# A hybrid attention layer in one kernel: reordering the twelve products behind the two value projections, their weight loads, and the engine of their low parts

## The chip, the core and the metric

The kernel runs on one NeuronCore of a Trainium2 chip. The metric is the device time of one execution in microseconds. The kernel before took 984.92 us (median of 3 runs, 984.27 to 985.51).

The engines have two names each, since the profile uses the short ones: TensorE (PE, with PEld for its weight loads), VectorE (DVE), ScalarE (ACT), GpSimd (POOL) and SyncE (SP). Each engine works through its own instructions strictly in the order of the program. SP issues nearly all DMAs, also in the order of the program: an issue that waits for a free buffer holds up every issue behind it.

## What is computed

One layer of a streaming encoder over 1,024 prompt rows and 64 sample rows of 1,024 columns, in float32. Cut to what matters here:

```python
h = rms_norm(x, norm_w) @ w_in                  # (1088, 1024) @ (1024, 6144)
sb_q, sb_k, sb_v, sb_z, cb_q, cb_k, cb_v, cb_z, g_sb, g_cb = split(h, SPLIT_POINTS)
o_sb = stick_breaking(sb_q, sb_k, sb_v)         # causal, plus caches for the sample rows
o_cb = band_attention(norm(cb_q), norm(cb_k), cb_v, rel_bias)
h = sigmoid(g_sb) * (o_sb * silu(z_sb)) @ w_proj_sb + sigmoid(g_cb) * (o_cb * silu(z_cb)) @ w_proj_cb
return x + h @ w_out, and the new k and v of both branches
```

The part that changes is the columns of `sb_v` (1024 to 1536) and `cb_v` (3072 to 3584) of the first product.

## The kernel before

**Split products.** TensorE multiplies in a fast float32 format with fewer bits. So each operand is kept as a high part (ScalarE rounds it, `A.activation(h, src, AF.Copy)`) and a low part (`src - h`), and each product is three matmuls: high by high, low by high, high by low.

**Seven products instead of eight.** From the values of a block on, the big products go by Strassen's scheme in Winograd's form: a 2 by 2 block product takes seven block products of sums of blocks. For x these sums are four tiles t0 to t3 (L180 to L227, `make_t`). t0 and t1 are made early. t1's unsplit value is stored to DRAM (`d_t1`), and the second half of `make_t` fetches it back eight times, k = 0 to 3 for t2 and then for t3: each of these eight jobs takes two subtractions or additions by VectorE, the high part by ScalarE and the low part by VectorE (`put_t`, L174). The generator is advanced at fixed places of the program, in the list `TJ` for its last nine steps: the first of them only fetches, the other eight are the jobs. A job of the kernel before fetches for the job two ahead, behind its own work, into the buffer that it has just read (two buffers, name `d`).

**The stage of this change** (L684 to L816) works on two "pairs" j: j = 0 is `sb_v`, j = 1 is `cb_v`. Of the seven products of each pair the first one (left block 0) has been made earlier, and the stage does five, numbered s = 1, 2, 6, 4, 5 by their left operand (`LEFT`, L712: s = 1 takes t1, s = 2 takes t0, s = 6 a half of x itself, s = 4 takes t2, s = 5 takes t3), while s = 0 is a small product of the sample rows alone (`sample`, 8 matmuls). The list `ORDER` (L713) fixes their sequence. A product has four parts, numbered 2c + tt, of 12 matmuls of 128 columns of weights by 256 columns each. At the head of each part `part((q, 2c+tt))` (L727) does what the program places there: sums of raw weight quarters (`sum_w`, VectorE), splits of a weight block into high and low part (`split_quad`, L510: high by ScalarE, low by GpSimd unless an engine is given), loads, and jobs of `make_t`. q is the place in `ORDER`. Behind each half c of a product, `evac_p` takes the result out of PSUM by VectorE, and for s of 3 and more `put_v` stores it.

**Weights.** A weight quarter of this stage is a tile of 128 by 4 by 256 float32 (512 KB), `quad[j, h, w]`: h the half of rows, w the half of columns. Written below as q_jhw. The pool `wpool` has two buffers `wraw` for them, `natx` one (`wrawx`), and a pool `rw` (r11, r00, r10), opened where the pools of the stage before are closed, has three more. The second pair's sums are made at (4, 0) to (4, 3). For splits, pool `wpool` and pool `natx` take turns.

**The stage ahead of it.** Products of the normed q and k columns run at L623 to L682, each followed by a norm, and three products later by a transpose (`post_nat`, L394: two transposes by TensorE, high part by ScalarE, low part by VectorE, stores at the fourth and eighth tile). The last four transposes fall into the parts (0, 0) to (0, 3). In them the PSUM tile is always `pk`, with one buffer.

**The opening.** At L540 to L610 tiles of x arrive (`load_x`), are normed and transposed, and the first products follow each tile. A list of places counted in matmuls (`SCALE`, `READY`, L562 to L591) says where the next x tile is scaled (`prep_a`, VectorE), transposed (`prep_b`) or its squares are summed (`prep_s`, ScalarE). Two loads of later weight blocks, `load_nat(1, 1)` and `load_nat(2, 0)`, stand ahead of this loop.

Of the kernel before, what the change touches and what calls it, by code (L numbers as in the profile page):

```python
# [34 lines left out]
def hybrid_step_kernel(ctx: ExitStack, tc: tile.TileContext, x_prompt, x_sample, c_sbk, c_sbv, c_cbk, c_cbv,  # L35
# [71 lines left out]
    turn = [0]  # L107

    def shifted(pool, shape, odd):

        o = 0 if turn[0] % 2 == odd else 32
        turn[0] += 1
        t = pool.tile([128, 1056], F32R, name="wlox", bufs=2)[:, o:o + 1024]
        if len(shape) == 4:
            return t.rearrange("p (s k n) -> p s k n", s=shape[1], k=shape[2])
        return t.rearrange("p (k n) -> p k n", k=shape[1])

    class Weights:
# [10 lines left out]
        def hi(self, key, cuts=1):  # L129
            raw, pool, shape, extra = self.raw[key]  # L130
            h = pool.tile(shape, F32R, name="whi" + extra, bufs=2)
# [3 lines left out]
            self.sp[key] = (h, None)  # L135

        def lo(self, key, eng=None):
# [3 lines left out]
            (eng or G).tensor_tensor(out=l, in0=raw, in1=h[:].bitcast(F32), op=OP.subtract)  # L141
# [36 lines left out]
    def make_t(tm, pool):  # L178
# [35 lines left out]
        fetch(*late[1])  # L214
        yield
        for e, (n, k) in enumerate(late):
            d = got[n, k]
            if n == 2:
# [6 lines left out]
            if e + 2 < 8:  # L225
                fetch(*late[e + 2])
# [3 lines left out]
    with ExitStack() as ph:  # L230
# [163 lines left out]
        def post_nat(i, t, qn):  # L394
# [4 lines left out]
            if t in (8, 4):  # L399
                hl[0] = p1h.tile([128, 2, 2, 576], F32R, name="hl", bufs=3)  # L400
            h = hl[0]
            n = 0 if raw1[:2] == (nb - 1, 7) else t % 3
            pt = (psQ.tile([128, 512], F32, name=f"b2{n - 1}")[:, :256].rearrange("p (j n) -> p j n", j=2) if n else
                  psK.tile([128, 2, 128], F32, name="pk"))
# [5 lines left out]
            A.activation(h[:, :, 0, o], pt[:, :, :r], AF.Copy)  # L410
            V.tensor_tensor(out=h[:, :, 1, o], in0=pt[:, :, :r], in1=h[:, :, 0, o].bitcast(F32), op=OP.subtract)
# [63 lines left out]
        def prep(n):  # L475
# [17 lines left out]
            elif s in (2, 4):  # L493
                t = natx.tile(shape, F32R, name="whix", bufs=2)
            else:
                t = wpool.tile(shape, F32R, name="whi" if s == 5 else "wlo", bufs=2)
# [13 lines left out]
        def split_quad(q, src, eng=None):  # L510
# [3 lines left out]
            h = pool.tile([128, 4, 256], F32R, name="whi" + x, bufs=2)  # L514
            A.activation(h, src, AF.Copy)
            l = shifted(pool, [128, 4, 256], 0) if x else pool.tile([128, 4, 256], F32R, name="wlo", bufs=2)
            (eng or G).tensor_tensor(out=l, in0=src, in1=h[:].bitcast(F32), op=OP.subtract)
# [35 lines left out]
        load_nat(1, 1)  # L553
        load_nat(2, 0)
# [10 lines left out]
        def early(at):  # L565
            if at in SCALE:
                p = SCALE.index(at) + 2
                prep_a(QO[p])
                if p + 3 < 9:
                    load_x(QO[p + 3])  # L570
            elif at in READY:
# [4 lines left out]
            elif at == 62:  # L576
                W.split((1, 0), V)
            elif at == 88:
# [44 lines left out]
        for i in range(2, nb):  # L623
# [4 lines left out]
            for ti, t in enumerate(TO):  # L628
# [14 lines left out]
                if ti in (3, 6):  # L643
                    h = ti // 6
                    if i + 1 < nb:
# [3 lines left out]
                        elif h == 0:  # L649
                            load_quad(0, 0, 1, wpool, "wraw", 2)  # L650
                        else:
                            load_quad(0, 1, 1, wpool, "wraw", 2)
# [3 lines left out]
                if (i, ti) == (nb - 1, 2):  # L656
                    for n in (1, 2):
                        made[n] = pn.tile([128, 4, 256], F32, name=f"made{n}", bufs=1)
                    sum_w(made[1], quad[0, 0, 1], quad[0, 1, 1], OP.add)
                if (i, ti) == (nb - 1, 4):  # L660
# [52 lines left out]
        ORDER = [(0, 1), (0, 2), (0, 6), (0, 0), (0, 4), (1, 1), (1, 2), (1, 6), (1, 0), (1, 4), (0, 5), (1, 5)]  # L713
        TJ = [(0, 2), (1, 1), (1, 3), (2, 1), (2, 3), (7, 0), (7, 2), (9, 0), (9, 2)]
        BANKS = {0: "2", 2: "1", 4: "3", 5: "2", 6: "1", 7: "1", 9: "2"}
        u, banks = {(0, "2"): s1t[0]}, {}

        def evac_p(j, s, c, ps):
            two = lambda v: v[:, 2 * c:2 * c + 2].rearrange("p t n -> p (t n)")
            if s < 3:  # L720
                V.tensor_tensor(out=two(u[j, "23"[s - 1]]), in0=ps, in1=two(u[j, "2"]), op=OP.add)
# [5 lines left out]
        def part(at):  # L727
# [3 lines left out]
            if at == (0, 2):  # L731
# [1151 lines left out]
```

## Time and profile before

| | |
|---|---|
| median of 3 runs | 984.92 us |
| lowest, highest | 984.27, 985.51 us |
| the profiled execution: its own time | 984.18 us |
| its span from first to last instruction | 982.0 us |
| TensorE busy (PE) | 954.2 us, 97% of the span |
| VectorE, ScalarE, GpSimd busy | 598.1, 499.3, 404.5 us (61%, 51%, 41%) |
| mean granted TensorE clock | 0.988 |
| DMA | 182.78 MB, mean 186 GB/s |

How to read it: all durations below come from the one profiled execution. Its time is 0.74 us below the median. Matmuls are pipelined, so the records of two neighbours overlap; the pace of a run of matmuls is its stretch of time divided by their number, not the duration of one. The granted clock is the share of the full TensorE clock in a stretch. In rows of waits the columns are total us, number of times and longest us. In rows of windows they are the length, then busy us and number of instructions of PE, PEld, DVE, ACT and POOL, then the granted clock, the DMA share and GB/s.

### The profile page before, as it was taken

How to read it: one execution, taken by the hardware profiler on the slowest of the kernel's cores; microseconds unless marked ns; L12 is line 12 of the kernel's file. 1: busy time of each engine (PE TensorE's matmuls, PEld its weight loads, DVE VectorE, ACT ScalarE, POOL GpSimd, SP SyncE). 2: the span in 40 equal slices, each digit the busy share in tenths (PEclk: the TensorE clock that was granted, in tenths of full speed). 3: DMA queues.
4: the chain of work that ended last, by engine and by line, in shares of the span. 5: the costliest groups of instructions: out<-in, count | busy, mean ns of one | idle time of the engine just before them, and what ended most of it. 6: DMA issues, size and time to landing. Idle time of an engine off the chain costs nothing.

```text
span 982.0 us, 20507 instructions
## 1 busy us (share of the span) xinstructions
PE 954.2 (97%) x7547; PEld 905.2 (92%) x7547; DVE 598.1 (61%) x1164; ACT 499.3 (51%) x1151; POOL 404.5 (41%) x395
## 2 busy tenths in 40 slices
PE   8899999598999999999999999999999999999998
PEld 8899999598999999999999988788888888999998
DVE  5646766765555555544332187778677766389745
ACT  6656766121444333343333276667887776465220
POOL 3156665262545465665543210001331111596641
PEclk9899999898999999999999999999999999999999
DMA  8537665526465655565532897789699851762642
GB/s 268 191 132 273 224 240 209 188 90 226 136 196 164 185 166 156 175 188 175 159 108 85 227 255 207 194 218 237 204 276 280 231 156 59 247 204 92 201 142 85
DMA packets 177705, 182.78 MB, mean 186 GB/s; under 512 B 30713, under 2 KB 160125, under 8 KB 177478
## 3 DMA queue, kind: packets, MB, share of 16 engines
q1 hardware_dynamic: 166182, 166.60, 56.9%
q10 hardware_dynamic: 8608, 8.20, 2.6%
q0 software_dynamic: 2816, 6.69, 2.1%
q8 instruction: 60, 0.98, 0.4%
q14 instruction: 39, 0.32, 0.1%
HBM read 117.79 MB, written 63.64 MB: 185 GB/s over the span
## 4 chain that ended last, share of the span: by engine, by line
PE 85%; DVE 5%; issue 3%; ACT 3%; DMA 1%; POOL 1%; ACTq 0%; DVEq 0%; POOLq 0%
PE b L943 30%; PE acc L560 8%; PE o L1465 7%; PE z L1368 7%; PE pt L1421 7%; PE b L1790 6%; PE acc L1219 5%; PE b L1261 5%; PE acc L1112 5%; PE b L811 3%; DMA xt<-in_x_prompt_dram 1%; PE b L560 1%; DVE d L222 1%; PE acc L1833 1%; DVE xn L312 1%
## 5 line engine op out<-in xcount | busy, mean ns | idle before, releaser
L1421 PE MATMUL pt<-ident,be 128*128 128x128 f32 (+1 forms) x568 | 87.1, 277 | 0.9 <-ACT wT L1430 0.6
L1390 DVE TENSOR_TENSOR_SCAN be<-be,imp 128x128 f32<-128x128 f32 (+7 forms) x64 | 82.8, 1341 | 8.3 <-ACT be L1371 8.3
L1368 PE MATMUL z<-ks,sq 128*128 128x320 f32 (+5 forms) x384 | 87.7, 338 | 0.0
L1430 ACT ACTIVATE wT<-pt 128x512 f32<-128x512 f32 (+3 forms) x123 | 57.2, 499 | 44.2 <-PE pt L1421 44.1
L1421 PEld LDWEIGHTS pt<-ident,be 128*128 128x128 f32 (+1 forms) x568 | 66.2, 140 | 13.8 <-issue 5.3
L943 PE MATMUL b<-xm,wlox 128*128 128x256 f32 (+1 forms) x336 | 76.0, 286 | 0.0
L951 DVE TENSOR_TENSOR u<-b,s 128x256 f32<-128x256 f32 (+1 forms) x56 | 24.3, 440 | 73.4 <-PE b L943 70.1
L1368 PEld LDWEIGHTS z<-ks,sq 128*128 128x128 f32 x384 | 63.5, 190 | 2.2 <-ACT be L1371 0.8
L1465 PE MATMUL o<-wT,vp 128*64 128x256 f32 (+1 forms) x608 | 64.1, 356 | 0.0
L1465 PEld LDWEIGHTS o<-wT,vp 128*64 128x64 f32 x608 | 40.3, 136 | 22.3 <-issue 5.4
L943 PEld LDWEIGHTS b<-xm,wlox 128*128 128x128 f32 x336 | 56.8, 188 | 0.0
L1393 ACT ACTIVATE be<-be,sm 128x640 f32<-128x640 f32 (+5 forms) x68 | 47.2, 694 | 17.7 <-DVE sm L1392 17.6
L1016 POOL DMA_DIRECT2D d_osb<-zt x20 | 10.8, 541 | 100.7 <-DVE zt L1479 43.9
L498 POOL TENSOR_TENSOR whix<-ws,whix 128x512 fp32r<-128x512 f32 x28 | 36.9, 1319 | 34.6 <-ACT whix L497 29.2
L1371 ACT ACTIVATE be<-z 128x384 f32<-128x384 f32 (+6 forms) x104 | 48.3, 521 | 3.4 <-PE z L1368 2.9
L498 POOL TENSOR_TENSOR wlo<-ws,wlo 128x512 fp32r<-128x512 f32 x28 | 38.9, 1388 | 25.5 <-ACT wlo L497 23.2
L1381 ACT ACTIVATE be<-be,sm 128x640 f32<-128x640 f32 (+5 forms) x68 | 47.3, 696 | 3.8 <-DVE sm L1373 3.3
L1261 PE MATMUL b<-og,whi 128*128 128x384 f32 (+1 forms) x192 | 46.7, 326 | 0.0
L845 ACT ACTIVATE hl<-u 128x256 f32<-128x256 f32 (+1 forms) x40 | 16.9, 431 | 55.3 <-DVE u L963 17.8
L943 PE MATMUL b<-t0h,whix 128*128 128x256 f32 (+1 forms) x224 | 44.6, 289 | 0.0
L943 PE MATMUL b<-t3h,whi 128*128 128x256 f32 (+1 forms) x224 | 44.5, 289 | 0.0
L386 ACT ACTIVATE qn<-qn,rsn 128x64 f32<-128x64 f32 (+1 forms) x144 | 38.2, 339 | 11.6 <-POOL rsn L294 11.4
(438 smaller groups left out, 3331.4 us busy)
## 6 DMA issues: line engine op xcount, KB each, us to landing
wraw<-in_w_in_dram SPq DMA_DIRECT2D x33, 512.0 KB, 4.9
wrawx<-in_w_in_dram SPq DMA_DIRECT2D x16, 512.0 KB, 4.3
sq<-d_qsbT SPq DMA_DIRECT2D x32, 192.0 KB, 5.0
sq<-d_qcbT SPq DMA_DIRECT2D x32, 192.0 KB, 4.9
xt<-in_x_prompt_dram SPq DMA_DIRECT2D x8, 512.0 KB, 4.6
d_kcbT<-hl SPq DMA_DIRECT2D x8, 512.0 KB
d_qcbT<-hl SPq DMA_DIRECT2D x8, 512.0 KB, 5.1
d_ksbT<-hl SPq DMA_DIRECT2D x16, 256.0 KB, 3.4
```

The lines of the kernel that those rows point to most:

```text
L498: G.tensor_tensor(out=t[:, 1], in0=src, in1=t[:, 0].bitcast(F32), op=OP.subtract)
L560: TE.matmul(ps, x, w, start=first, stop=last, skip_group_check=i < 2)
L943: TE.matmul(ps[:, :m], w[:, hl_, k], right[s](x)[:, k, a:b], start=s < 3 and k == 0 and e == 0, stop=k == 3 and e == 2, skip_group_check=s ...
L1112: TE.matmul(ps[:, :b - a], w[:, k], xk(x, k)[:, a:b], start=k == 0 and n == 0, stop=k == KT - 1 and n == 2)
L1219: TE.matmul(ps[:, :e - a], w[:, p, cw], g[:, a:e], start=m % 12 == 0, stop=m % 12 == 11)
L1261: TE.matmul(pp[uu][:, :n], w[:, p, uu * 128:uu * 128 + 128], g[:, a:e], start=p == 0 and m == 0, stop=p == NPAIR - 1 and m == 2)
L1368: TE.matmul(z[:, :m], s[:, e, q0:q0 + 128], ks[:, h, o + x:o + y], start=(e, h) == parts[0], stop=(e, h) == parts[-1])
L1390: V.tensor_tensor_scan(be[:r, n - 1::-1], be[:r, n - 1::-1], im[:, ::-1], 0.0, op0=OP.mult, op1=OP.max)
L1421: TE.transpose(pt[:kr, x, :r], be[:r, kb * 128:kb * 128 + kr], ident[:r, :r])
L1430: A.activation(w[:, sl:sl + m, q0:q0 + r], pt[:, :m, :r], AF.Copy)
L1465: TE.matmul(o[hd * 64:hd * 64 + 64, c0:c1], vv[:kr, kb, hd * 64:hd * 64 + 64], wT[b, p, j, hd, s // 4][:kr, s % 4, c0:c1] if j < 4 else wT ...
L1790: TE.matmul(ps[:, t], left[s](xs_, k)[:, ts_], wt_[:, k], start=s < 3 and t == k == e == 0, stop=k == 3 and e == 2, skip_group_check=s > 2 ...
```

## The change

- `ORDER`: the second pair's products s = 2, 1 and 6 come ahead of the first pair's s = 4, which needs t2; the second pair's s = 5 comes ahead of the first pair's. `TJ` spreads the eight jobs differently, and each job fetches for the next one ahead of its own work.
- The second pair's sums and splits move forward to (1, 3) to (4, 1). The splits of places 2, 4 to 10 give their low part to VectorE; those of q_001 and q_011 (the keys 3 and 11) stay with GpSimd.
- Loads: q_011 is loaded ahead of q_001, q_111 takes its buffer in the stage before, q_011 is loaded a second time at (7, 1) (in place of q_111 before), q_101 comes at (0, 3), and `rw` holds q_100, q_110 and two sums.
- `evac_p` takes the results of the second pair's s = 2 out of PSUM together with those of s = 1. Some banks change.
- The last four transposes of `post_nat` use the two-buffer tile `pt`.
- In the opening, `load_nat(1, 1)` moves behind a load of an x tile at 24 matmuls, and `load_nat(2, 0)` to 62 matmuls.
- High parts named `whix` get the same alternating offset of 32 columns that low parts named `wlox` had.

```diff
 def fetch / late half of make_t
         fetch(*late[0])
-        fetch(*late[1])
         yield
         for e, (n, k) in enumerate(late):
             d = got[n, k]
+            if e < 7:
+                fetch(*late[e + 1])
...
-            if e + 2 < 8:
-                fetch(*late[e + 2])
             yield
 post_nat
-            n = 0 if raw1[:2] == (nb - 1, 7) else t % 3
-            pt = (psQ.tile(...b2{n - 1}...) if n else psK.tile([128, 2, 128], F32, name="pk"))
+            if raw1[:2] == (nb - 1, 7):
+                pt = psT.tile([128, 4, 128], F32, name="pt")
...
 opening
-        load_nat(1, 1)
-        load_nat(2, 0)
...
                     load_x(QO[p + 3])
+                if p == 2:
+                    load_nat(1, 1)
...
             elif at == 62:
                 W.split((1, 0), V)
+                load_nat(2, 0)
 the stage before
-                            load_quad(0, 0, 1, wpool, "wraw", 2)
+                            load_quad(0, 1, 1, wpool, "wraw", 2)
                         else:
-                            load_quad(0, 1, 1, wpool, "wraw", 2)
+                            load_quad(0, 0, 1, wpool, "wraw", 2)
...
                     sum_w(made[1], quad[0, 0, 1], quad[0, 1, 1], OP.add)
+                    load_quad(1, 1, 1, wpool, "wraw", 2)
 the stage
-        ORDER = [(0, 1), (0, 2), (0, 6), (0, 0), (0, 4), (1, 1), (1, 2), (1, 6), (1, 0), (1, 4), (0, 5), (1, 5)]
-        TJ = [(0, 2), (1, 1), (1, 3), (2, 1), (2, 3), (7, 0), (7, 2), (9, 0), (9, 2)]
-        BANKS = {0: "2", 2: "1", 4: "3", 5: "2", 6: "1", 7: "1", 9: "2"}
+        ORDER = [(0, 1), (0, 2), (0, 6), (0, 0), (1, 2), (1, 1), (1, 6), (0, 4), (1, 0), (1, 4), (1, 5), (0, 5)]
+        TJ = [(0, 2), (1, 1), (2, 3), (4, 2), (5, 0), (6, 2), (7, 0), (7, 3), (9, 0)]
+        BANKS = {0: "2", 2: "1", 4: "3", 5: "2", 6: "1", 7: "3", 9: "2"}
...
-                V.tensor_tensor(out=two(u[j, "23"[s - 1]]), in0=ps, in1=two(u[j, "2"]), op=OP.add)
+                for e in ((s,) if j == 0 else (1, 2) if s == 1 else ()):
+                    V.tensor_tensor(out=two(u[j, "23"[e - 1]]), in0=banks[j, e, c], in1=two(u[j, "2"]), op=OP.add)
...
-            if at == (0, 2):
+            if at == (0, 0):
                 split_quad(3, quad[0, 0, 1])
...
-            elif at == (0, 3):
+            elif at == (0, 2):
                 sum_w(quad[0, 1, 0], quad[0, 1, 0], made[2], OP.subtract)
...
+            elif at == (0, 3):
+                sum_w(quad[0, 0, 0], quad[0, 0, 0], quad[0, 0, 1], OP.subtract)
+                load_quad(1, 0, 1, wpool, "wraw", 2)
             elif at == (1, 0):
...
-                split_quad(2, quad[0, 1, 0])
-            elif at == (1, 1):
-                sum_w(quad[0, 0, 0], quad[0, 0, 0], quad[0, 0, 1], OP.subtract)
-                split_quad(4, quad[0, 0, 0])
-                load_quad(1, 0, 1, wpool, "wraw", 2)
+                split_quad(2, quad[0, 1, 0], V)
             elif at == (1, 2):
...
-                for h, w in ((1, 1), (0, 0), (1, 0)):
+                for w, h in ((0, 0), (0, 1)):
                     load_quad(1, h, w, rw, f"r{h}{w}", 1)
...
+            elif at == (1, 3):
+                for n in (1, 2):
+                    made[n] = rw.tile([128, 4, 256], F32, name=f"r{n}", bufs=1)
+                sum_w(made[1], quad[1, 0, 1], quad[1, 1, 1], OP.add)
+                split_quad(4, made[1], V)
+            elif at == (2, 1):
+                sum_w(made[2], made[1], quad[1, 0, 0], OP.subtract)
+            elif at == (2, 2):
+                split_quad(5, made[2], V)
             elif at == (4, 0):
-                sum_w(quad[1, 1, 1], quad[1, 0, 1], quad[1, 1, 1], OP.add)
-                made[2] = rw.tile([128, 4, 256], F32, name="r2", bufs=1)
-                sum_w(made[2], quad[1, 1, 1], quad[1, 0, 0], OP.subtract)
-                split_quad(5, made[2])
-            elif at == (4, 2):
-                split_quad(6, quad[1, 1, 1])
+                sum_w(quad[1, 1, 0], quad[1, 1, 0], made[2], OP.subtract)
+            elif at == (4, 1):
+                split_quad(6, quad[1, 1, 0], V)
+            elif at == (5, 1):
+                split_quad(7, quad[0, 0, 0], V)
+            elif at == (5, 3):
                 made[3] = natx.tile([128, 4, 256], F32, name="wrawx", bufs=1)
                 sum_w(made[3], quad[1, 0, 0], quad[1, 0, 1], OP.subtract)
-            elif at == (4, 3):
-                sum_w(quad[1, 1, 0], quad[1, 1, 0], made[2], OP.subtract)
-                split_quad(7, quad[1, 1, 0])
             elif at == (6, 0):
-                split_quad(8, quad[1, 0, 1])
                 rwx.close()
                 open_t((3,))
-            elif at == (7, 0):
-                split_quad(9, made[3])
-            elif at == (7, 3):
-                split_quad(10, quad[0, 1, 1])
-                load_quad(1, 1, 1, wpool, "wraw", 2)
+                split_quad(8, quad[1, 0, 1], V)
+            elif at == (6, 3):
+                split_quad(9, made[3], V)
+            elif at == (7, 1):
+                split_quad(10, quad[1, 1, 1], V)
+                load_quad(0, 1, 1, wpool, "wraw", 2)
+            elif at == (7, 2):
                 load_raw(0)
-            elif at == (9, 2):
-                split_quad(11, quad[1, 1, 1])
+            elif at == (9, 1):
+                split_quad(11, quad[0, 1, 1])
                 load_raw(1)
                 load_raw(2)
```

More of the change, by code (lines that the diff above doesn't have):

```diff
@@ L105, in hybrid_step_kernel, with shifted @@
     wpool = ctx.enter_context(tc.tile_pool(name="wp", bufs=2))
[L107 to L113, printed above, removed]
+    turn = {}
+    def shifted(pool, shape, odd, name="wlox"):
+        n = turn[name] = turn.get(name, 1) + 1
+        o = 0 if n % 2 == odd else 32
+        t = pool.tile([128, 1056], F32R, name=name, bufs=2)[:, o:o + 1024]
         if len(shape) == 4:
@@ L130, in hi @@
             raw, pool, shape, extra = self.raw[key]
-            h = pool.tile(shape, F32R, name="whi" + extra, bufs=2)
+            h = shifted(pool, shape, 0, "whix") if extra else pool.tile(shape, F32R, name="whi", bufs=2)
             for j in range(cuts):
@@ L134, in hi @@
                 A.activation(h[:, k], raw[:, k], AF.Copy)
-            self.sp[key] = (h, None)
+            self.sp[key] = (h[:], None)
         def lo(self, key, eng=None):
@@ L140, in lo @@
             l = shifted(pool, shape, 0) if extra else pool.tile(shape, F32R, name="wlo", bufs=2)
-            (eng or G).tensor_tensor(out=l, in0=raw, in1=h[:].bitcast(F32), op=OP.subtract)
+            (eng or G).tensor_tensor(out=l, in0=raw, in1=h.bitcast(F32), op=OP.subtract)
             self.sp[key] = (h, l)
@@ L401, in post_nat @@
             h = hl[0]
-            n = 0 if raw1[:2] == (nb - 1, 7) else t % 3
-            pt = (psQ.tile([128, 512], F32, name=f"b2{n - 1}")[:, :256].rearrange("p (j n) -> p j n", j=2) if n else
-                  psK.tile([128, 2, 128], F32, name="pk"))
+            if raw1[:2] == (nb - 1, 7):
+                pt = psT.tile([128, 4, 128], F32, name="pt")
+            elif t % 3:
+                pt = psQ.tile([128, 512], F32, name=f"b2{t % 3 - 1}")[:, :256].rearrange("p (j n) -> p j n", j=2)
+            else:
+                pt = psK.tile([128, 2, 128], F32, name="pk")
             for j in range(2):
@@ L409, in post_nat @@
             o = slice(c, c + r)
-            A.activation(h[:, :, 0, o], pt[:, :, :r], AF.Copy)
-            V.tensor_tensor(out=h[:, :, 1, o], in0=pt[:, :, :r], in1=h[:, :, 0, o].bitcast(F32), op=OP.subtract)
+            A.activation(h[:, :, 0, o], pt[:, 0:2, :r], AF.Copy)
+            V.tensor_tensor(out=h[:, :, 1, o], in0=pt[:, 0:2, :r], in1=h[:, :, 0, o].bitcast(F32), op=OP.subtract)
             dst = (d_kT if isk else d_qT)["cb"]
@@ L493, in prep @@
             elif s in (2, 4):
-                t = natx.tile(shape, F32R, name="whix", bufs=2)
+                t = shifted(natx, shape, 0, "whix")
             else:
@@ L513, in split_quad @@
             pool, x = ((wpool, ""), (natx, "x"))[n % 2]
-            h = pool.tile([128, 4, 256], F32R, name="whi" + x, bufs=2)
+            h, l = (shifted(pool, [128, 4, 256], 1, part + x) if x else
+                    pool.tile([128, 4, 256], F32R, name=part, bufs=2)[:] for part in ("whi", "wlo"))
             A.activation(h, src, AF.Copy)
-            l = shifted(pool, [128, 4, 256], 0) if x else pool.tile([128, 4, 256], F32R, name="wlo", bufs=2)
-            (eng or G).tensor_tensor(out=l, in0=src, in1=h[:].bitcast(F32), op=OP.subtract)
+            (eng or G).tensor_tensor(out=l, in0=src, in1=h.bitcast(F32), op=OP.subtract)
             comb[q] = h, l
@@ L649, in hybrid_step_kernel @@
                         elif h == 0:
+                            load_quad(0, 1, 1, wpool, "wraw", 2)
+                        else:
                             load_quad(0, 0, 1, wpool, "wraw", 2)
-                        else:
-                            load_quad(0, 1, 1, wpool, "wraw", 2)
                             load_quad(0, 0, 0, natx, "wrawx", 1)
@@ L800, in hybrid_step_kernel @@
             for c in range(2):
-                if s != 5:
-                    banks[j, c] = None
                 for tt in range(2):
@@ L805, in hybrid_step_kernel @@
                     if tt == 0 and s != 5:
-                        banks[j, c] = psF.tile([128, 512], F32, name="acc") if q == 1 else bank_of(BANKS[q], c)
-                    ps = banks[j, c]
+                        banks[j, s, c] = psF.tile([128, 512], F32, name="acc") if q == 1 else bank_of(BANKS[q], c)
+                    ps = banks[j, 4 if s == 5 else s, c]
                     o = ps[:, 256 * tt:256 * tt + 256]
```

## The prediction

> **What bounds the kernel now.** I read the chain that ended last first, then who waits for TensorE's work, then the changed stretches alone.
>
> ```profile
> PE 85%; DVE 5%; issue 3%; ACT 3%; DMA 1%; POOL 1%; ACTq 0%; DVEq 0%; POOLq 0%
> ```
>
> TensorE carries the chain, so a change is worth what it takes out of TensorE's idle time and slow clock. The waits of PE between 155 and 245 us, the stretch of the ten products:
>
> ```profile
> PE b L811 <- ACT t2h L175: 8.9, 3, 6.2
> PE b L811 <- ACT t3h L175: 4.0, 1, 4.0
> PE pk L406 <- DVE hl L411: 1.5, 1, 1.5
> ```
>
> The same stretch as one window, one window behind the long wait and one around the start of the second; then two pieces of the chain:
>
> ```profile
> 161.22:244.13 82.91, 67.82 (x522) 65.39 (x523) 52.29 (x59) 19.46 (x30) 30.21 (x14) 0.90 0.57 186
> 186.59:193.42 6.83, 0.62 (x2) 0.33 (x2) 2.27 (x4) 0.66 (x1) 0.00 (x0) 0.50 0.57 214
> 224.13:227.55 3.42, 1.40 (x12) 1.20 (x11) 3.42 (x3) 0.86 (x1) 2.34 (x1) 1.00 1.05 355
> 67.37 2.83 PE acc L560 x24
> 244.13 14.94 PE b L943 x120
> ```
>
> The stage ends at 244.13, where the next products (L943) begin. Its 512 matmuls and 8 transposes at the undisturbed pace of 0.118 us (2.83 per 24) need some 61.3 us, and take 82.9. PE is idle for 82.9 - 67.8 = 15.1 of them, and the rest of the 21.6 is the clock: granted 0.50 after the long wait and 0.90 over the stage. It waits first for t2 in the first pair's s = 4, then for t3 in its s = 5. The third loss, 1.5 us, lies just ahead of 161.22: the first of the last four transposes waits for the single buffer `pk`.
>
> The other stretch is the opening, in the chain:
>
> ```profile
> 0.75 4.02 DMA xt<-in_x_prompt_dram
> 15.77 7.09 DMA xt<-in_x_prompt_dram
> 22.96 1.15 ACT sq L303 x2
> 24.11 0.96 ACT whi L134
> 25.15 1.08 issue
> 27.11 1.32 PE pt L322 x8
> 28.43 5.09 PE b L560 x24
> 33.76 0.87 PE pt L322 x8
> ```
>
> The fifth x tile takes 7.09 us to land, where the very first took 4.02. Then ScalarE's squares, its high part, VectorE's low part and scaling follow, and only then the transposes at 27.11. The 24 matmuls from 28.43 take 5.09 us, 0.212 each: half the clock.
>
> **The opening.** SP's issues, the last work of ScalarE ahead of its wait, and three windows:
>
> ```profile
> 13.25 0.39 SPq L126 DMA_DIRECT2D wrawx<-in_w_in_dram  x1
> 13.68 0.50 SPq L126 DMA_DIRECT2D wraw<-in_w_in_dram  x1
> 15.77 0.37 SPq L256 DMA_DIRECT2D xt<-in_x_prompt_dram  x1
> 20.31 0.60 ACT L328 ACTIVATE xm<-pt 128x512 fp32r<-128x512 f32 x1
> 22.75:26.16 3.41, 0.21 (x2) 0.01 (x1) 1.07 (x1) 2.64 (x5) 0.74 (x2) 1.00 0.06 25
> 26.16:29.58 3.42, 2.47 (x13) 2.22 (x14) 2.32 (x5) 1.50 (x3) 0.00 (x0) 0.50 0.49 143
> 29.58:32.99 3.41, 3.41 (x17) 3.41 (x17) 2.12 (x3) 1.64 (x4) 0.74 (x2) 0.50 0.22 88
> ```
>
> The x tile queues behind 1 MB of weights that are split only at 88 and 166 matmuls, while its own place is 24. The change puts it first; its issue stays at 15.77 (its buffer comes free then). At the first tile's 4.02 it lands by 19.8, and ScalarE takes it up when `xm` is done: the second of two 0.5 us steps behind 20.31, so at 20.8. Everything up to the transposes moves by 22.96 - 20.8 = 2.1 us. In the windows PE does 0.21 us, then 2.47 of 3.42, and is still at 0.50 in the third; with PE back at 25.0 the second window is full. If one full window lifts the clock, half speed ends at 29.6 instead of 33. That would save one more us. The same chain then sets the next tile's transposes (33.76 before): PE back at 25.0, 1.3 of transposes, and again 1.15 of squares, 0.96 of high part, 1.08 of low part and 0.88 to the transposes make 30.4. Between ends of 2.0 (clock as before) and 3.3 I take **-3.0**, since from there to 159 every wait is counted from PE's own places. The moved loads are covered: issued near 16 and 20 and landing in 4 to 7 us by the two rows above, they are there long before their splits; uncovered, each would cost its landing.
>
> **The start of the stage.** With two buffers the transposes start 1.5 us earlier, at 159.7: **-1.5**. The last of the four still needs the norm of the last tile, which ScalarE ends about as PE gets there; the split of key 3 moved to (0, 0) puts 1 us of ScalarE ahead of it.
>
> **The stage.** PE no longer meets s = 4 early, so both waits in the first three rows go. What is late next? The change puts eight low parts onto VectorE and keeps its sums, jobs and evictions, so I lay out VectorE's queue. Prices:
>
> ```profile
> 159.60 1.23 DVE L517 TENSOR_TENSOR wlox<-made,whix 128x1024 fp32r<-128x1024 f32 x1 [1.42 <-ACT whix L515]
> 193.84 1.22 DVE L438 TENSOR_TENSOR r<-wraw,r 128x1024 f32<-128x1024 f32 x1
> 179.49 0.71 DVE L219 TENSOR_TENSOR d<-d,xa 128x544 f32<-128x544 f32 x1
> 182.33 0.68 DVE L721 TENSOR_TENSOR made<-acc,made 128x512 f32<-128x512 f32 x1
> 182.93 0.71 DVE L219 TENSOR_TENSOR d<-d,xa 128x544 f32<-128x544 f32 x1
> 225.31 2.73 DVE L222 TENSOR_TENSOR d<-xm,d 128x544 f32<-128x544 f32 x1
> 225.13 2.34 POOL L517 TENSOR_TENSOR wlox<-wraw,whix 128x1024 fp32r<-128x1024 f32 x1 [3.12 <-ACT whix L515]
> L515 ACT ACTIVATE whi<-wraw 128x1024 fp32r<-128x1024 f32 x3 | 3.1, 1047 | 0.0
> ```
>
> A sum or a low part holds VectorE for 1.15 (its end overlaps the next), 1.1 more where it waits for a high part just begun; a job 2.85 (179.49 to 182.33, ScalarE's high part inside); an eviction 0.6. A two-input operation beside GpSimd's low part takes 2.73 instead of 0.71, so moving those parts off GpSimd also removes such meetings; they are left out of the list except for key 3 at the start. Landings (the second and third row are from the DMA issues of 160 to 245 us, with the median time to landing):
>
> ```profile
> 160.86 0.38 SPq L508 DMA_DIRECT2D made<-in_w_in_dram  x1
> made<-in_w_in_dram SPq DMA_DIRECT2D x1, 512.0 KB, 4.4
> d_qcbT<-hl SPq DMA_DIRECT2D x4, 512.0 KB, 5.1
> 179.00 0.33 SPq L211 DMA_DIRECT2D d<-d_t  x1
> 179.50 1.48 SPq L508 DMA_DIRECT2D r<-in_w_in_dram  x3
> 181.03 0.50 SPq L757 DMA_DIRECT2D u<-d_s  x1
> 182.43 3.76 SPq L211 DMA_DIRECT2D d<-d_t  x2
> 190.39 0.72 DVE L219 TENSOR_TENSOR d<-d,xa 128x544 f32<-128x544 f32 x1 [3.94 <-DMA d<-d_t]
> ```
>
> From 179.00 to the landing at 190.3 the queue moved 272 + 3 x 512 + 512 + 272 = 2,592 KB in 11.3 us; loads land in the order of issue. That is the price of a backlog: 0.44 us per 100 KB, latency inside.
>
> On the old clock, without the opening's 3 us: q_010, issued at 160.86 as now, lands at 165.3, and key 3's low part on GpSimd ends soon after. From 165.6 VectorE does two sums, an eviction, the low part of key 2 (170.0), job 0 (172.8), an eviction, and waits for q_101, which queues behind two stores of 512 KB: issued near 167.4, they take 5.1, and q_101 another 2.2, so 174.7. Then: sum and split 4 to 178.2, sum and split 5 to 182.3 with two evictions in its gaps, job 1 and an eviction 185.7, sum and split 6 189.2, jobs 2 and 3 194.9, split 7 196.3, two evictions, a sum, two evictions 199.8, split 8 201.0, an eviction, job 4 204.4, split 9 205.9, an eviction, job 5 209.3, split 10 210.7, an eviction, job 6 and an eviction 214.8. Job 7 needs a fetch that SP issues only behind the second load of q_011, which waits for split 10's low part. At 210.9 that puts 512 (q_011) + 512 (stores) + 512 (raw 0) + 272 KB on the queue: 7.9 us, landing 218.9. Job 7 ends at 221.7, and the eviction behind it at 222.3.
>
> PE, unhindered from 159.7, wants split 4 at 178.5 (there by 0.3), split 5 at 184.2, split 6 at 189.8 (by 0.6), split 7 at 195.5: 0.9 late. Split 9 at 203.0: 3.0 late. It reaches the second pair's s = 5 at 213.2, which adds onto banks that VectorE must have read: 222.4, a wait of **9.2 us**, in place of waits of 6.2 and 4.0. It then runs below full clock for two windows (2.3 us lost, from the 0.50 rows) and ends the remaining 96 + 16 matmuls (13.2 us) at **237.9**, against 244.13: -6.2, of which 1.5 were counted above, so **-4.7**. The last stores' buffers hold back the fold of the samples and, behind it on ScalarE, the third weight block of the next stage: +0.3, between 0 and 1.
>
> The bank swaps, the deferred eviction (two in a row, counted) and the offset of `whix` add no instruction. The q_111 load in the stage before follows a sum there; it delays no wait that I see.
>
> Sum: -3.0 - 1.5 - 4.7 + 0.3 = -8.9. The profiled execution took 984.18 (span 982.0 and 2.2 around it), so 975.3 of its own; the median shown lies 0.74 above it, so the forecast is **976.0**.
>
> **A rule weighed.** The row has GpSimd's low part at 2.34 and VectorE's at 1.23. The Trainium skill (GPSIMD Engine Reference, 4.1 Engine selection) recommends VectorE for such elementwise work since GpSimd takes about twice as long for two inputs; this trace agrees on the ratio. Taken as the whole answer, the rule makes each late part sooner and gives the first rival below; the list above says that VectorE's queue is already the late one.
>
> **Rivals.** *VectorE keeps up* (or the last fetch lands early): with none of these waits the stage would end at 159.7 + 61.3 = 221.0 at best, total 984.2 + 0.7 - 3.0 - 23.1 = 959; without the fetch's 4.1 us and its slow clock alone, 970. For it: the prices carry small overlaps, and the fetch might overtake. Against: 190.39 shows landings in order, and the queue of VectorE from 165.6 has no slack. Chance 0.15, 959 to 971. *A smaller gain*: the opening's load was not the end of its wait, or VectorE runs 3 to 5 us later still: 979 to 983; chance 0.15. *Nothing*: the waits only change place, within 0.2% (2 us, about what a measurement of this kernel can tell from no change); 0.04. *Slower*: sums wait in VectorE's queue for raw quarters, where nothing behind can pass. Ahead of q_101 stand 0.5 MB of weights and some 2.4 MB of stores and fetches; each us by which it lands later than 174.7 moves the whole list, and past 184 the gain is gone. At 0.44 us per 100 KB it would take 2 MB more; landing at 187 gives 988. Chance 0.05.
>
> **The numbers.** The forecast has 0.61. Its own range is 972 to 980: opening 1, VectorE's list 1.5, the fetch 2, the clock 1.2 each way. Half of the first rival and half of the second are taken in as well, so 966 to 981, which leaves out some 2 in 10. Faster 0.91, same 0.04, slower 0.05.
>
> **What would show it.** Right: PE back near 25 in the opening and full clock by 29.6; no wait for `pk`; none for t2h; then waits of PE for VectorE's low parts (splits 7 and 9) and a long one near 210 (after the shift) on the second pair's s = 5, with VectorE waiting for `d` by DMA just before; GpSimd nearly idle in the stage. Wrong: x still landing after 22; PE without a wait of 5 us in the last four products; or a PE wait for t2, or VectorE idle for us before 175.

## The result, and the profile after

After took 974.49 us (median of 4 runs, 973.41 to 976.03), before 984.60 beside it (4 runs); the ratio is 0.9901, 95% interval 0.988 to 0.9923. Faster, by 9.7 us (7.6 to 11.8) at that ratio. The profiled execution of after took 975.09 (span 973.2), 9.09 less than that of before; the forecast was 976.0.

The chain of after by engine (in this profile it leads back only to 192.8 us, so its shares can't be set beside those of before), then the waits of PE from 155 to 240 us (total us, times, longest):

```profile
PE 71%; DMA 3%; ACT 2%; DVE 2%; issue 1%; SPq 1%; ACTq 0%; DVEq 0%
```

```profile
PE b L820 <- ACT wlox L499: 9.2, 1, 9.2
PE b L820 <- issue: 2.2, 1, 2.2
```

The rows for t2h, t3h and `pk` are gone. Both labels are misleading, since they name what ended last by the profile: what PE got can be seen among VectorE's operations (start, duration, operation, and in brackets the idle time before it):

```profile
192.82 1.22 DVE L519 TENSOR_TENSOR wlox<-wrawx,whix 128x1024 fp32r<-128x1024 f32 x1 [0.23 <-ACT whix L518]
193.96 0.68 DVE L726 TENSOR_TENSOR u<-b,u 128x512 f32<-128x512 f32 x1
194.68 0.69 DVE L726 TENSOR_TENSOR made<-b,u 128x512 f32<-128x512 f32 x1
...
215.24 0.73 DVE L223 TENSOR_TENSOR d<-xm,d 128x544 f32<-128x544 f32 x1 [2.40 <-DMA d<-d_t]
...
218.09 1.28 DVE L729 TENSOR_TENSOR o<-b,made 128x512 f32<-128x512 f32 x2
```

PE's first wait ends at 195.57, behind the eviction of 194.68: the first pair's s = 4 takes the bank "3" that the second pair's s = 2 has filled, and its deferred eviction stands behind the low part of split 7. The second ends at 218.87, when job 7 is done and the first of the two evictions of 218.09 as good as read; L499, which its label names, makes a weight block of the next stage, which this product doesn't read.

The stage as one window, from the first of the last four transposes (157.49) to the first matmul of the next stage (233.90); then the windows around the two waits and two of the opening (length, then busy us and count of PE, PEld, DVE, ACT, POOL, then the granted clock, DMA share, GB/s):

```profile
157.49:233.90 76.41, 65.00 (x522) 64.54 (x521) 50.49 (x68) 20.18 (x35) 7.22 (x6) 0.91 0.57 184
192.02:195.53 3.51, 1.37 (x12) 1.17 (x10) 3.25 (x5) 1.71 (x2) 0.00 (x0) 1.00 0.00 1
195.53:198.94 3.41, 3.37 (x16) 3.40 (x17) 3.38 (x5) 0.00 (x0) 0.00 (x0) 0.50 0.01 2
219.42:222.84 3.42, 3.42 (x18) 3.42 (x17) 0.00 (x0) 0.00 (x0) 2.63 (x2) 0.50 0.24 65
21.44:24.86 3.42, 1.79 (x16) 1.60 (x15) 1.70 (x2) 2.64 (x5) 0.74 (x2) 1.00 0.97 282
24.86:28.27 3.41, 2.29 (x21) 2.14 (x22) 2.25 (x5) 1.77 (x5) 0.00 (x0) 1.00 0.63 191
```

The stage takes 76.41 us. Between the same two points it took 82.75 in before (161.22 to 243.97): 6.3 of the 9.1 us. PE idles 11.4 us in it; GpSimd is down to 7.2 us of work, VectorE has 50.5. The opening, in the timeline:

```profile
16.04 0.37 SPq L255 DMA_DIRECT2D xt<-in_x_prompt_dram  x1
21.59 1.07 ACT L302 ACTIVATE sq<-xt 128x1024 f32<-128x1024 f32 x1 [0.41 <-DMA xt<-in_x_prompt_dram]
25.75 0.43 PE L321 MATMUL pt<-ident,xn 64*128 64x64 f32 x4 [2.52 <-DVE xn L311]
31.32 0.96 PE L321 MATMUL pt<-ident,xn 128*128 128x128 f32 x5 [1.31 <-DVE xn L311]
```

The x tile is taken 5.55 us after its issue (7.19 before), PE is back at 25.75 (27.11 before), and the clock stays at 1.00. A new wait of 1.31 us gives part of it back: PE is now ahead of the next tile's chain through ScalarE and VectorE. The transposes of 25.75 are those of the sample rows' tile (64x64 in the row), whose squares ScalarE had taken at 17.32. They don't read the fifth x tile and stand behind it by the order of the lists alone: VectorE scales the sample rows behind a weight block's low part, which waits for ScalarE's high part, which stands behind the fifth tile's squares. Another order of these was not tried. Behind the opening, after leads by 2.0 us, and with the `pk` wait gone the stage starts 3.7 us sooner (157.49 against 161.22).

From the stage's end on, before takes 738.1 us more to the end of its span and after 739.3. Other kernels below with the same code there take 737.6 to 740.2 (e11, which loads later for the next stage, 743.2), so nothing is read from that.

### The profile page after: what moved, and what is told of

It is laid out like the page before. It is cut to its first block, busy times and chain, and to the rows that moved or that the text cites. A ratio compares the mean times of both kernels' runs of the same rounds, so it can differ in the third digit from the quotient of the medians.

```text
span 973.2 us, 20499 instructions
## 1 busy us (share of the span) xinstructions
PE 950.6 (98%) x7547; PEld 903.8 (93%) x7547; DVE 595.6 (61%) x1172; ACT 498.7 (51%) x1151; POOL 382.4 (39%) x387
## 4 chain that ended last, share of the span: by engine, by line
PE 71%; DMA 3%; ACT 2%; DVE 2%; issue 1%; SPq 1%; ACTq 0%; DVEq 0%
PE b L952 30%; PE o L1474 7%; PE z L1377 7%; PE pt L1430 7%; PE b L1799 6%; PE acc L1228 5%; PE b L1270 5%; PE acc L1121 2%; PE b L820 1%; DMA sq<-d_qsbT 1%; DMA ks<-d_ksbT 1%; PE acc L1842 1%; DVE acc L1315 0%; DMA d<-d_t 0%; PE acc L878 0%
## 5 line engine op out<-in xcount | busy, mean ns | idle before, releaser
L1430 PEld LDWEIGHTS pt<-ident,be 128*128 128x128 f32 (+1 forms) x568 | 66.2, 140 | 13.7 <-issue 5.1
```

Of the source, the lines that this page charges most:

```text
L1430: TE.transpose(pt[:kr, x, :r], be[:r, kb * 128:kb * 128 + kr], ident[:r, :r])
```

## The experiments

*The theory* at this point: the order of the products frees TensorE from the wait for t2, and then VectorE's list from 163 to 218 us, work and standing still together, sets the stage. *The rivals*: the fetch of job 7 alone sets the long wait; the gain is that of the engine that makes the low parts; the opening and the transposes' buffer carry what they were priced at. Each ratio below is to runs of before on the same chip, where the median of before was 983.92 (e1 to e4), 984.55 (e5 to e8), 985.08 (e9 to e11) and 984.04 (e12). "Stage" is the stretch of the windows above.

| kernel | median us | ratio (95%) | stage us | PE idle in it |
|---|---|---|---|---|
| before | 984.60 | 1 | 82.75 | 15.1 |
| after | 974.49 | 0.9901 (0.988 to 0.9923) | 76.41 | 11.4 |
| e1 before, new opening | 982.76 | 0.9986 (0.9977 to 0.9995) | 81.88 | |
| e2 before, two buffers | 983.28 | 0.9995 (0.9987 to 1.0004) | 82.71 | |
| e3 after, low parts on GpSimd | 976.12 | 0.9919 (0.9905 to 0.9933) | 77.49 | 13.9 |
| e4 before, low parts on VectorE | 983.64 | 0.9998 (0.9987 to 1.001) | 81.72 | 14.4 |
| e5 after, two operations more | 977.51 | 0.993 (0.9918 to 0.9943) | 79.55 | 13.0 |
| e6 after, fetches two ahead | 972.70 | 0.988 (0.9866 to 0.9893) | 74.19 | 9.7 |
| e7 after, low parts deferred | 977.65 | 0.9935 (0.9922 to 0.9947) | 79.39 | 13.5 |
| e8 after, interleaved | 965.63 | 0.981 (0.9796 to 0.9824) | 66.61 | 4.2 |
| e9 after, later weight load | 976.82 | 0.9924 (0.9907 to 0.9942) | 77.89 | 12.1 |
| e10 e8, sums exchanged | 965.80 | 0.9811 (0.9796 to 0.9826) | 66.88 | 3.7 |
| e11 e10, products exchanged | 968.64 | 0.9838 (0.9821 to 0.9854) | 66.13 | 2.4 |
| e12 after, old opening | 978.14 | 0.9934 (0.9921 to 0.9947) | 77.19 | 12.7 |

Each stage's length comes from one profile. After, e9 and e12 have the same code in the stage and take 76.41, 77.89 and 77.19, so a difference of up to 1.5 us from after says nothing; e3 lies within these three, e5 to e8, e10 and e11 outside. Two ratios differ beyond their noise from about 0.0025 on.

**e1: the opening alone.**

```diff
-        load_nat(1, 1)
-        load_nat(2, 0)
...
+                if p == 2:
+                    load_nat(1, 1)
...
                 W.split((1, 0), V)
+                load_nat(2, 0)
```

> Before with the opening's load order alone (two weight loads behind the fifth x tile). The two traces put the shift behind the opening at 2.0 us (the norms' transposes start at 156.38 before and 154.33 after), and in the stage of the ten products everything hangs on places that move with it. Theory: 2.0 us off, 982.6. As recorded: 3.0 off, 981.6. Rival: a later wait takes it up, 984.6.

Measured: 1.4 us off (0.5 to 2.3). In this profile ScalarE takes the x tile at 22.91, 6.54 us after its issue, and two windows run at half clock as in before. So with the same edit ScalarE takes the tile 5.55 us after its issue in one profile and 6.54 in another; e12 and e9 come back to that.

**e2: the transposes' two buffers alone** (in before, `pt` for `pk` in the last four transposes).

> Before with two buffers for the last four transposes alone. As recorded (a term of its own): 1.5 us off, 983.1. Theory now: TensorE is 1.5 us earlier at the first pair's s = 4 and waits there 1.5 us longer, because t2 hangs on fetches and on VectorE and not on the transposes: the wait for pk goes, the first wait for t2 grows from 6.2 to about 7.7, and the time stays at 984.6.

Measured: 0.5 off (-0.4 to 1.3), so the recorded 1.5 is out. The waits of PE in this profile:

```profile
PE b L814 <- ACT t2h L175: 8.6, 3, 5.9
PE b L814 <- ACT t3h L175: 4.2, 1, 4.2
PE b L814 <- POOL wlox L520: 1.3, 2, 1.0
```

`pk` is gone, but the wait for t2 has not grown (5.9), so my theory of where the time goes was wrong too. New is a wait of 1.0 us at 173.15: PE comes sooner to the third product and finds key 2's low part not yet done by GpSimd. The saved wait is mostly spent at the next late operand.

**e3: the new order with the old engine, and e4: the old order with the new engine.**

```diff
 e3, in after, for keys 2 and 4 to 10:
-                split_quad(2, quad[0, 1, 0], V)
+                split_quad(2, quad[0, 1, 0])
 e4, in before, for the same keys:
-                split_quad(2, quad[0, 1, 0])
+                split_quad(2, quad[0, 1, 0], V)
```

> After with the eight low parts of the stage back on GpSimd, the new order of products, loads and sums kept. Theory (VectorE's list is the bound, and its two-input operations are held for as long as GpSimd's low part runs, 2.73 against 0.71 us): eight low parts of 1.15 leave VectorE, but each may hold it for up to 2 us, so the list is no shorter: 974 to 982, with rows of 2 us and more on VectorE. Rival (only the number of operations on VectorE counts): the list is 9.2 us shorter and TensorE's waits of 2.2 and 9.2 go: 963 to 966.

> Before with the same eight low parts (keys 2 and 4 to 10) on VectorE, its order of products, loads and sums kept. Theory (the order is needed, since the first pair's s = 4 asks for t2 as fifth product at 181, and VectorE's list cannot have the four jobs done by then): the first wait for t2 stays within 2 us of its 6.2 and the time lies within 3 us of 984.6. Rival (the engine is all): all of the stage's gain without the opening's, 974.5 + 2.0 = 976.5.

Measured: e3 takes 976.12, e4 983.64. All of the change but the engine gives nearly all of the gain; the engine by itself gives nothing (ratio 0.9998), and its waits are those of before. By e1 and e2 the opening and the buffer are small parts of that, so the bulk falls to the order with the sums, loads and jobs that go with it; these weren't tried one by one.

```profile
PE b L811 <- ACT t2h L175: 8.7, 3, 6.0
PE b L811 <- ACT t3h L175: 4.2, 1, 4.2
PE pk L406 <- DVE hl L411: 1.4, 1, 1.4
```

In e3's timelines, VectorE's list has lost eight low parts of 1.15, but some two-input operations grow while GpSimd runs one:

```profile
180.25 2.43 POOL L519 TENSOR_TENSOR wlox<-r,whix 128x1024 fp32r<-128x1024 f32 x1 [2.31 <-ACT whix L518]
180.28 2.97 DVE L221 TENSOR_TENSOR d<-d,xm 128x544 f32<-128x544 f32 x1
196.22 3.40 DVE L440 TENSOR_TENSOR wrawx<-r,wraw 128x1024 f32<-128x1024 f32 x1 [1.31 <-POOL wlox L519]
```

The operation of 180.28 takes 2.97 instead of 0.73: it ends 0.57 behind GpSimd's low part, as if it had begun only then. The list ends at 219.97 + 1.28, 63.3 us behind its stage's start, in after 61.9 (218.09 + 1.28). So the list is no shorter without the eight parts, as expected: VectorE is busy 52.15 us in the stage, in after 50.49, with eight operations fewer. Part of what TensorE waits longer comes back as clock (0.96, in after 0.91):

```profile
157.97:235.47 77.50, 63.61 (x523) 62.47 (x522) 52.15 (x60) 20.16 (x35) 26.45 (x14) 0.96 0.56 181
```

The Trainium skill (SBUF — State Buffer, section "SBUF: two separate sides") says that the two engines share a port pair as an exclusive lock: of a VectorE operation with two SBUF inputs and a GpSimd operation that reads SBUF, the one that starts first has it for its whole instruction, and the other blocks. The row of 180.28 agrees; it starts 0.03 us behind GpSimd's.

**e5: two operations of 1.15 more on VectorE.**

```diff
                 split_quad(8, quad[1, 0, 1], V)
+                for _ in range(2):
+                    V.tensor_tensor(out=comb[8][1], in0=quad[1, 0, 1], in1=comb[8][0].bitcast(F32), op=OP.subtract)
```

> After with the low part of key 8 computed three times over on VectorE (the same output, two operations of 1.15 us more, at 199). Theory (VectorE's list from 195 to 218 is the bound): all behind it moves by 2.3, the fetch of job 7 too, since it waits for VectorE's stores; TensorE's wait of 9.2 becomes 11.5 and the time 976.8. Rival (a DMA sets that wait: job 7's fetch had VectorE waiting 2.4 us): the wait absorbs the two operations and the time stays at 974.5.

Measured: 977.51, ratio 0.993 against 0.9901, and the stage is 3.1 us longer. VectorE's wait for job 7's fetch stays at 2.32 (2.40 in after), so it absorbs nothing. The waits of PE:

```profile
PE b L822 <- ACT wlox L499: 9.3, 1, 9.3
PE b L822 <- issue: 2.8, 1, 2.8
PE b L822 <- DVE wlox L519: 0.8, 1, 0.8
```

The long wait did not become 11.5: PE lost 1.6 us more in idle time, part of it (the 0.8) already ahead of split 9's product, and the rest in one more window at half clock (17.1 us of the stage, in after 13.7). The sum, 2.9 us by the ratios with some 2.5 either way, fits the 2.3 of the list theory, though not by the longer wait that it forecast. The rival, no loss at all, is out.

**e6: the fetches two ahead, at each job's end, as in before.**

```diff
         fetch(*late[0])
+        fetch(*late[1])
...
-            if e < 7:
-                fetch(*late[e + 1])
...
             put_t([t(n, s, k) for s in range(2)], d)
+            if e + 2 < 8:
+                fetch(*late[e + 2])
```

> After with the sums' reloads fetched two ahead at the end of each job, as before the change, instead of one ahead at the start of each. Theory: job 7's fetch leaves at 207.5, behind job 5's low part, instead of 210.9, and is there when VectorE comes to it at 212.8: its wait of 2.4 goes and TensorE's wait of 9.2 falls to 6.8; against that q_101 lands up to 1.2 us later behind the second fetch (272 KB ahead of it), which pushes VectorE's list from 172. Net 1.2 to 2.4 off, 972.1 to 973.3. Rival (the queue is full of stores, and the landing does not follow the issue): 974.5.

Measured: 972.70; the stage is 2.2 us shorter, VectorE no longer waits for job 7's `d`, and the long wait is 6.75. Against it, q_101 comes later: VectorE stands 1.41 us ahead of its sum (0.69 in after) and the first wait is 2.96. Both were expected. Of the 9.2 us the fetch thus carries at most 2.5 (0.7 of these because TensorE comes to the wait later), the list the rest. So the fetch one ahead, a part of the change, is worse than what before had; the two ratios alone (0.0021 apart) would not show it.

**e7: the jobs' low parts deferred behind the next job's operations.**

```diff
-            put_t([t(n, s, k) for s in range(2)], d)
+            A.activation(t(n, 0, k), d, AF.Copy)
+            wait.append((n, k, d))
+            while wait and (len(wait) > 1 or e in (3, 7)):
+                a, b, v = wait.pop(0)
+                V.tensor_tensor(out=t(a, 1, b), in0=v, in1=t(a, 0, b).bitcast(F32), op=OP.subtract)
+            if e < 7:
+                fetch(*late[e + 1])
```

> After with each late job's low part put behind the next job's two operations (jobs 3 and 7 end at once), so that VectorE does not stand for ScalarE's high part. Six waits of 0.72 to 0.83 leave VectorE's list, 4.4 us; but a fetch waits for the low part whose buffer it takes and leaves later, so that VectorE stands for d instead, above all in job 3, which follows job 2 at once, and in job 7. Theory (list is the bound, fetches next): 1 to 3.5 us off, 971 to 973.5, with the waits for d grown from 2.4. Rival (only the last fetch matters): no gain or slower, 974.5 to 976.5.

Measured: 977.65, slower than after, beyond both expectations. The waits of VectorE:

```profile
DVE wlox L523 <- ACT whix L522: 3.9, 4, 1.7
DVE d L221 <- DMA d<-d_t: 3.6, 1, 3.6
DVE wlo L523 <- ACT whi L522: 3.5, 3, 1.3
DVE r L444 <- DMA d<-d_t: 3.0, 1, 3.0
DVE d L218 <- DMA d<-d_t: 2.9, 1, 2.9
```

The waits in jobs are gone, but three DMA waits of 9.5 us in all stand in their place (3.1 in after). Each low part holds the buffer that a later fetch takes, so jobs 3 and 7 stand for `d` (2.9 and 3.6). VectorE also comes to q_101's sum sooner than q_101 (3.0; the row's label names a fetch, which that sum doesn't read), which lands no earlier than it did. And the wait for a high part moved into the splits (up to 1.7), since ScalarE now makes the job's high part first.

**e8: the list interleaved.** Jobs are cut in two (operations and high part, then low part and a fetch two ahead), and splits too; the later ones run:

```diff
+                split_quad(9, made[3], "hi")
+                job()
+                split_lo(9, made[3], V)
+                job()
```

The first line makes the split's high part alone, the first `job()` a job's two operations and its high part, the second its low part and the next fetch. So each low part on VectorE has another operation ahead of it while ScalarE works. Key 5's and 10's low parts only move behind later operations; jobs come a place or two sooner.

> After with VectorE's list rearranged from the first job on: each split's high part is issued ahead of a job's two operations and its low part between those and the job's own low part, so that nearly no operation stands for ScalarE; the fetches leave two ahead, at each job's end; the jobs come earlier by a place or two. Theory (the list is the bound): 2.4 us of the fetch and some 8 of the waits for ScalarE (0.59 to 1.25 in three splits, eight of 0.72 in the jobs) leave it between 172 and 218; TensorE's waits of 2.2 and 9.2 shrink to 0 to 3 and the slow clock behind them costs little: 962 to 966. Rival (the landings of q_101, the quarters and the fetches bind as soon as the list is shorter): 968 to 972.

Measured: 965.63, ratio 0.981. The window of the stage, PE's one wait left, then VectorE around the job of 197:

```profile
158.81:225.41 66.60, 62.39 (x522) 62.22 (x521) 50.05 (x68) 20.73 (x35) 7.21 (x6) 0.97 0.66 211
```

```profile
PE b L854 <- issue: 4.2, 1, 4.2
```

```profile
197.37 0.72 DVE L223 TENSOR_TENSOR d<-xm,d 128x544 f32<-128x544 f32 x1
198.13 0.73 DVE L224 TENSOR_TENSOR d<-d,xb 128x544 f32<-128x544 f32 x1
198.77 1.22 DVE L529 TENSOR_TENSOR wlox<-wrawx,whix 128x1024 fp32r<-128x1024 f32 x1
199.91 0.72 DVE L227 TENSOR_TENSOR t3l<-d,t3h 128x544 fp32r<-128x544 f32 x1
```

VectorE does the same 50 us of work as in after (50.05 and 50.49) and the stage is 9.8 us shorter, 7.6 of these against e6, which has the fetches two ahead alone: what bound it was not how much VectorE does but that it stood still between. No row here has a wait in brackets. PE's wait that is left ends behind an eviction (209.96 to 210.65) that had itself stood 0.53 us for a store's buffer. This version beats both kernels.

**e9: the weight load behind the sixth x tile, and e12: after with the old opening.** In e9 `p == 2` becomes `p == 3`; e12 undoes the edit of e1.

> After with the first of the two moved weight loads put behind the sixth x tile instead of the fifth (from 16.4 to about 20.9 us). In the profiles so far ScalarE takes the fifth tile 5.3 to 6.5 us after its issue with the change, and 6.9 to 7.3 without it, against 4.0 for the very first tile. Theory (the 512 KB issued 0.4 us behind the tile share the transfer with it): it is there 4.0 to 4.6 us after its issue, ScalarE takes it when its last work is done (0.5 to 1 us sooner), and the time is 0.5 to 1.5 us lower, 973 to 974. Rival (what stands ahead of it, two stores, or the first weights, sets the landing): 5.3 to 6.5 us again and 974.5.

> After with the two weight loads of the opening back in their old place, ahead of the loop; all else as in after. In the profiles so far the first of the last four transposes starts at 157.5 to 159.7 with the moved loads (mean of nine kernels 158.3) and at 159.5 without them where it has two buffers (one kernel). Theory (the moved loads are worth 1.2 us of the tile's landing, and a half-clock window more or less by the run): 1.3 us slower than after, 975.8, with the start at 159 to 160.5. As recorded: 3.0 slower, 977.5. Rival (only in the opening, taken up later): 974.5.

Measured: e9 takes 976.82, no better than after, and ScalarE takes the tile 5.73 us after its issue; so in this profile the load behind it is not what it waits for. What else sets it was not tried. e12 takes 978.14: the opening is worth 0.0033 of the ratio there, 3.2 us, with some 2.5 either way from the two intervals. From all profiles: with the moved loads ScalarE takes the tile 4.9 to 6.5 us after its issue (after, e1, e3, e5 to e8, e10, e11; mean 5.7), without them 6.4 to 7.3 (before, e2, e4, e12; mean 6.9). In e10 and e11 (4.9 and 5.2) ScalarE was itself busy until then, so the tile may have landed sooner. Behind it none to two windows run at half clock: none in after, one in six of these profiles, two in e1, e8 and e9; two without the edit in three, one in e12.

**e10 and e11: q_101's load between the two sums, and the last two products exchanged.**

```diff
 e10 and e11
+                sum_w(quad[0, 0, 0], quad[0, 0, 0], quad[0, 0, 1], OP.subtract)
+            elif at == (0, 3):
+                load_quad(1, 0, 1, wpool, "wraw", 2)
                 sum_w(quad[0, 1, 0], quad[0, 1, 0], made[2], OP.subtract)
 e11
-... (1, 0), (1, 4), (1, 5), (0, 5)]
+... (1, 0), (1, 4), (0, 5), (1, 5)]
```

> The interleaved kernel with the sums of key 4's quarter and key 2's quarter exchanged and q_101's load between them, so that the load's buffer is free sooner. Theory: the load leaves 2 to 3 us sooner than 167.5, VectorE's wait of 1.9 for q_101 goes, and the remaining wait of TensorE of 4.2 ahead of the tenth product falls to about 2.3: 963.5. Rival (GpSimd's low part of key 3 holds that sum, or the stores and fetches on the queue set the landing): no gain, 965.6.

> The same, and the last two products exchanged: the first pair's s = 5 first, whose banks were read several us sooner, its quarter reloaded behind key 8's split and split with GpSimd's low part, and key 11 split on VectorE behind the jobs. One low part of 1.15 and the evictions of the ninth product then stand behind job 7. Theory (the list up to t3 is the bound): the wait of 4.2 falls to 0.5 to 1.5, no half-clock window or one: 960.5 to 962.5. Rival (the reload lands late behind stores, or GpSimd's low part holds VectorE by 2 us): a wait of 3 to 5 us, 964 to 967.

Measured: e10 965.80, e11 968.64. In e10 the load leaves at 166.62, 8.84 us behind the stage's start (8.67 in e8): the two stores ahead of it on SP end only at 166.5, so the buffer was not what it waited for, and the rival holds. In e11 the stage itself is shortest (66.13), but VectorE's timeline shows

```profile
202.16 0.69 DVE L737 TENSOR_TENSOR o<-b,made 128x512 f32<-128x512 f32 x1 [2.77 <-DMA out_dram<-o]
202.76 2.19 DVE L223 TENSOR_TENSOR d<-xm,d 128x544 f32<-128x544 f32 x1
```

an eviction that waits for a store's buffer, and a job's operation that runs beside GpSimd's low part (2.19 for 0.72). Worse, the next stage's raw blocks are loaded later (210.47, in e10 from 203.24 on), and TensorE waits 0.9 and 0.8 us for them; the next stage takes 301.3 us instead of 298.5. Together with later losses that weren't traced, the exchange costs 2.8 us.

## Why the prediction was right, step by step

**The sum (-8.9).** The mechanism came as forecast: no wait for t2, VectorE's list as the bound, a long wait on the second pair's s = 5 with VectorE standing for a fetch just before, GpSimd nearly idle. That the sum fits to 0.2 us of the profiled execution (975.3 forecast, 975.09 measured) is luck: by the two profiles the opening gave 1.0 less than its term and the rest of the kernel took 0.9 more, while the stage gave 1.6 more and its start 0.2 more.

**The opening (-3.0).** Right in place, too large by a third: 2.0 in the profile, 1.4 by e1, 3.2 by e12. The step that failed is the landing: "at the first tile's 4.02 it lands by 19.8". ScalarE had it after 5.55 us, and after 4.9 to 6.5 over the runs. Why it is slower than the first tile stays open; e9 speaks only against the load behind it. The chain to the next tile's transposes was expected at 30.4 and came at 31.32. The clock did better than expected (no window at 0.50), which is a matter of the run.

**The buffer (-1.5).** The wait did go, but e2 shows that by itself it is worth 0.5, since PE then waits for key 2's low part. In after that low part is VectorE's and done by 167.8, so it can count there: the stage starts 1.7 us sooner than the opening's 2.0 explain. It wasn't measured by itself in after.

**The stage (-4.7).** It became 6.3 us shorter. VectorE's list was right within 0.3 us as far as split 10: 51.0 us behind the stage's start by the list, 51.3 in the profile (208.80). Two steps failed. The first is the fetch: "SP issues only behind the second load of q_011, which waits for split 10's low part". q_011 went out at 205.99, ahead of that low part, since it took the buffer of key 8. The fetch left later than forecast, at 210.89 behind two stores and a raw quarter, but landed within 4.33 us by the chain, not 7.9, since q_011 had landed by then (4.6 us after its issue). The price itself held: from the first of the two stores (209.43) to the landing (215.21) the queue moved 1,296 KB in 5.8 us, and 0.44 per 100 KB makes 5.7. So job 7 and the eviction behind it ended 1.3 us sooner: PE starts 61.4 us behind the stage's start, by the list 62.7. The second is TensorE's part. The list had it wait 0.9 for split 7 and 3.0 for split 9; it waited 2.2 and 0. It stood for bank "3", which TensorE's part of the list left out, and the half-clock window that this wait brought (the row of 195.53) made it late enough for split 9. The long wait was forecast at 9.2 and measured at 9.22, which is partly luck: both its ends came 1.3 us sooner.

**The engine.** The prediction put the eight low parts on VectorE's list as work and set no price on the meetings with GpSimd that go in exchange. e3 shows that the two cancel: the move is worth 1.1 us of the stage, no more than profiles of the same stage differ by, and by the ratios nothing that can be told from zero. The rule weighed (the Trainium skill, GPSIMD Engine Reference, 4.1 Engine selection) is right per operation, 2.43 us against 1.22 here, and says little of the stage.

**The hold-back (+0.3).** The next stage took 297.5 instead of 297.1, about as forecast: before, e1, e2 and e4 take 297.1 to 297.2, after, e9 and e12 297.5 to 297.7, but e5 and e7 297.1 again. That the samples' fold makes the difference wasn't shown.

**The rivals.** VectorE did not keep up, by 9.2 us; e8 shows that with another order of its own list it nearly could have. q_101 landed by 172.0, so the slower case was far off.

## What to carry to other kernels

When the list of an in-order engine is the bound, lay it out as work and standing still: here 50 us of work stayed the same while the stage went from 76.4 to 66.6 us, once each operation that needs another engine's result had an operation of other use ahead of it and the fetches went two ahead (which alone gave 2.2). Deferring the operation alone isn't enough, since it holds the buffer of the next fetch: feed the list first, with fetches two ahead. And a wait taken away is worth only the distance to the next late operand, so price small waits together and in the new order, not one by one.

## What was not expected of the hardware

**The clock fell after windows in which TensorE was busy for 40%.** A window with 1.37 us of 3.51 busy was followed by one at 0.50 (the rows of 192.02 and 195.53), as was one with 1.40 of 3.42 in before (the prediction's row of 224.13, with 0.50 from 227.55 on), one with 1.79 of 3.42 by one at 1.00 (21.44 and 24.86). The Trainium skill (TensorE: Matmul & The Clock Gate, "What's actually happening") speaks of an idle window; in this trace a partly busy one is enough. A wait of 2.2 us thus cost 1.6 more: the 24 matmuls from 195.57 to 200.14 took 4.57 us, where 24 at full clock have 2.99 from first start to last end. In e3, with 13.9 us of idle time in shorter pieces, the clock of the stage was 0.96 against 0.91 in after with 11.4, so there the form of the waits, or where the windows fell, counted as much as their sum.

**The landing of one and the same load varies by 1.2 us** between executions of kernels with the same opening: where ScalarE stood waiting for the fifth x tile, it came 5.3 to 6.5 us after its issue (seven kernels), a spread as large as the shift of the mean by the edit.
